# FFN input projection on one NeuronCore: the two blocks multiplied in full give way to first products of seven pairs ahead

## The chip, the cores and the metric

The kernel runs on 1 core of one Trainium2 chip. A core has a matrix engine (TensorE, PE in the profile), a vector engine (VectorE, DVE), a scalar engine (ScalarE, ACT), GpSimd (POOL), and a sync engine (SyncE, SP) that issues nearly all DMA transfers here. Each engine works through its own instruction list in the order in which the program was written, and the engines wait for each other by semaphores. The metric is the device time of one execution in microseconds (us); less is better.

## The reference, cut to what matters

One decoder block on 1024 tokens of width 1024: RMS norm and input projection, a dilated attention mixer and a convolution mixer, merged and projected (the "mix" projection), then a SwiGLU FFN with a hidden width of 2816. The change lies where the mix ends and the FFN begins:

```python
x = x + rms_norm(merged @ w_mix_out[l], g_post_mix[l])
h = rms_norm(x, g_pre_ffn[l])
gate, up = jnp.split(h @ w_ffn_in, 2, axis=-1)       # 2 x 2816 columns
x = x + rms_norm((jax.nn.silu(gate) * up) @ w_ffn_out, g_post_ffn[l])
```

All values are float32. The kernel splits a float32 operand into a rounded high part and a low part (`split`, `both`, `part`: a ScalarE copy makes the high part, a VectorE subtraction the low part) and replaces each product by three: high x high, high x low, low x high.

## The kernel before, in words

**Stages around the change.** Eight mix tiles of 128 tokens come first (loop with line 1697): tiles 0 and 1 together, then 2 to 7 one by one, each into two PSUM banks; one tile is 48 matrix products of 512 columns. The weights of all eight contraction steps (16 slots) and the left operands stay in SBUF until tile 7 is done. After each tile `mix_norm` runs beside the following products: squares (L1396), the first norm and the residual (L1403, L1407), a store of the new x (L1414), the second norm (L1418, L1420), which gives `hn`. After tile 3 the four `hn` of the first 512 tokens are transposed on TensorE in eight groups of four (L1428), scaled (L1434) and split (`split`, L1286 and L1287); after tile 7 the same is done for the last 512 tokens.

**The FFN input.** It runs over 22 blocks j of 128 hidden columns, each with a gate and an up half. From j = 2 on a block is one pair of weight tiles: `winograd` treats the 2 x 2 blocks (gate/up by first/second half of the contraction) and 2 x 2 halves of the activations (halves of the contraction by halves of the tokens) with 7 block products in place of 8. Each block product is `prod`: 4 contraction steps of 3 matrix products (lines 334 to 336). It needs sums of weights (`quarters`, steps 0 to 5) and sums T1 to T4 of the activations (`quarter_sums`, L391 to L401), which need all 1024 tokens. Blocks j = 0 and 1 are multiplied in full (`ffn_half`): 8 `unit` calls of 24 matrix products each (lines 318 to 320), the first four with the first 512 tokens alone.

**What sets the order.** The program order is written by hand. After every three matrix products of `unit` and `prod` (and every three or six of the mix) `tick()` is called; `later(n, step)` emits a step n ticks on, and background generators (`bg`) are advanced one step a tick unless they have yielded a number of ticks to skip. What is emitted at a tick stands at that place in the list of its engine. `load_ahead` issues weight loads on SP's queue. Slots: 42 tiles of 128x1024 (`slot`, NSLOT), 3 of the same size for rows (`ring`), 11 of half that size (`half`), and the 8 PSUM banks. A tile's slot comes free after its last use in program order, and what takes the slot next waits for that use.

Of the kernel before, what the change touches and what calls it, by code (L numbers as in the profile page):

```python
# [40 lines left out]

EARLY = 1

PLAIN = 2

LAST = 5
NSLOT = 42
# [11 lines left out]
def f(ap):  # L59
    return ap.bitcast(F32)  # L60


class Build:
# [104 lines left out]
    def flush(self, i):  # L168
        while any(p[0] <= i for p in self.pieces):
            self.one_piece()  # L170

    def load_ahead(self, i):
        while self.sent < min(len(self.jobs), i + 1):
# [3 lines left out]
            self.nc.sync.dma_start(self.raw[j][:, :n], src)  # L177
            self.sent += 1
# [33 lines left out]
    def quarters(self, i, c):  # L212


        nc = self.nc
        if c == 0:
            self.hl[i] = {}
        o = self.hl[i]
        r1, r2 = self.raw[i - 1], self.raw[i]
        a11, a12, a21, a22 = r1[:, :H], r1[:, H:], r2[:, :H], r2[:, H:]  # L220
        add = self.wsplit.tensor_tensor
        l, r = slice(0, H), slice(H, 2 * H)
        if c == 0:
            h, w = self.both(r1)
            o["A11"], o["A12"] = (h[:, l], w[:, l]), (h[:, r], w[:, r])
        elif c == 1:
            self.s12 = self.ring()
            add(self.s12[:, l], a21, a22, op=OP.add)
            add(self.s12[:, r], self.s12[:, l], a11, op=OP.add)  # L229
        elif c == 2:  # L230
            h, w = self.both(self.s12)
            o["S1"], o["S2"] = (h[:, l], w[:, l]), (h[:, r], w[:, r])
        elif c == 3:
# [3 lines left out]
            self.s12 = None  # L237
        elif c == 4:
            h, w = self.both(self.s34)
            o["S3"], o["S4"] = (h[:, l], w[:, l]), (h[:, r], w[:, r])  # L240
            self.s34 = None
        else:
            x = self.slot(F32R)
            nc.scalar.copy(x[:, l], a22)
            add(x[:, r], a22, f(x[:, l]), op=OP.subtract)
            o["A22"] = (x[:, l], x[:, r])
            del self.raw[i], self.raw[i - 1], self.hl[i]

    def queue_split(self, i):
        while self.queued < min(self.sent, i + 1):  # L250
# [88 lines left out]
    def winograd(self, W, T, f11, f12, f21, f22):  # L339
# [31 lines left out]
        self.prod(X, W["A22"], T["T4"], False, True)  # L371
        if rest:
            rest()
        f21(X)

    def quarter_sums(self, B, blocks):
# [906 lines left out]
    def split(self, src, n):  # L1283
        nc = self.nc
        s = self.slot(F32R)
        nc.scalar.copy(s[:, :n], src)  # L1286
        nc.vector.tensor_tensor(s[:, 512:512 + n], src, f(s[:, :n]), op=OP.subtract)  # L1287
        return s

    def rhs(self, ops):  # L1290
        return lambda kt: (ops[kt][:, :512], ops[kt][:, 512:])
# [118 lines left out]
    def mix_norm(self, tt, banks, x):  # L1410
        nc = self.nc
        x2 = self.ring()
        yield from self.residual(banks, x, self.g_mix, x2)
        nc.sync.dma_start(self.d_x2[tt], x2)  # L1414
        yield 1
        hn = self.slot()
        ss = self.tiny(4, "ss", 4)
        nc.scalar.activation(hn, x2, AF.Square, scale=ROOT, accum_out=ss[:, 0:1])  # L1418
        r = self.rstd_rows(ss[:, 0:1], self.eps_rms)
        nc.scalar.activation(hn, x2, AF.Copy, scale=r)  # L1420
        self.hn[tt // 4].append(hn)
        if tt % 4 == 3:
            yield 8
            op, y = [], None
            for kt in range(8):
                ps = self.bank("s")
                for i in range(4):
                    nc.tensor.transpose(ps[:, i * 128:(i + 1) * 128], self.hn[tt // 4][i][:, kt * 128:(kt + 1) * 128], self.ident)  # L1428
# [4 lines left out]
                y = x[:, (kt % 2) * H:(kt % 2 + 1) * H]  # L1433
                nc.scalar.activation(y, ps, AF.Copy, scale=self.col(C_PREF + kt))  # L1434
                self.h2f[tt // 4].append(y)
                yield 1
            op.append(self.split(y, H))
            self.h2[tt // 4] = op
            self.hn[tt // 4] = None

    def row_gain(self, src):
        g = self.slot()
# [4 lines left out]
def build(ctx, tc, aps):  # L1447
# [5 lines left out]
    def job(src, n=1024, kind=""):  # L1453
        J.append((src, n, kind))
        return len(J) - 1

    NQ, NK = 0, 12
    NU, NG, NGA, NGC = 24, 32, 40, 48
    def pair(a, b):
# [10 lines left out]
          for hg in range(2) for g in range(3)}  # L1470
# [4 lines left out]
    fi = [(job(aps["w_fi"][j], kind="row1" if j >= PLAIN else ""),  # L1475
           job(aps["w_fi"][FT + j], kind="row2" if j >= PLAIN else "")) for j in range(FT)]
# [147 lines left out]
    for n, hf in [(n, hf) for hf in range(2) for n in range(3)] + [(n, hf) for n in range(3, 8) for hf in range(2)]:  # L1624
# [2 lines left out]
            mg[n] = nxt  # L1627
            nxt = gate_load(B.d_gc[n + 1]) if n < 7 else (gate_load(B.d_ga[0]), gate_load(B.d_gc[0]))
        if B.tags["g"] == 2 and B.weighed == 4:
            B.banks(g=6, s=2)  # L1630
# [13 lines left out]
    for e in B.merges:  # L1644
        B.finish(e)
    if B.tags["g"] == 2:
        B.banks(g=6, s=2)
    mop = [[None] * 8, [None] * 8]

    rest = lambda: None  # L1650
# [18 lines left out]
    rest()  # L1669
    B.OT = None  # L1670

    W = [B.weights(mx[0])]
    B.g_mix = B.row_gain(aps["g_mix_row"])
    B.hn, B.h2, B.h2f = [[], []], [None, None], [[], []]
    norms = []

    def load_x(tt):
# [6 lines left out]
    xt = {0: load_x(0), 1: load_x(1)}  # L1684
    for tiles in ((0, 1), (2,), (3,), (4,), (5,), (6,), (7,)):
        banks = {tt: (B.bank(), B.bank()) for tt in tiles}
        for kt in range(KT):
            if len(W) == kt:
                B.ahead = int(kt < KT - 1)
                W.append(B.weights(mx[kt]))  # L1690
            for tt in tiles:
                m = mop[tt // 4]
# [48 lines left out]
            sub(s4, a12, a11, op=OP.subtract)  # L1741
            spill(p, "S4", s4)

    def ffn_half(j, hf, W):
        o = B.half()
        ps = B.unit(W[0], B.rhs(B.h2[hf]), KT)
        nc.scalar.activation(o, ps, AF.Silu)
        ps = B.unit(W[1], B.rhs(B.h2[hf]), KT)
        nc.vector.tensor_tensor(o, ps, o, op=OP.mult)
        held[j, hf] = o  # L1750

    B.wsplit = nc.vector
    Ws = []
    for j in range(PLAIN):
        Ws.append((B.weights(fi[j][0]), B.weights(fi[j][1])))
        ffn_half(j, 0, Ws[j])
    B.finish(norms[-1])
    B.g_mix = None
    h2 = [[(x[:, :H], x[:, H:]) for x in y] for y in B.h2]
    qs = B.bg(B.quarter_sums(B.h2f, (h2[0][:4], h2[0][4:], h2[1][4:])))  # L1760
    h2 = None
    for j in range(PLAIN):
        ffn_half(j, 1, Ws[j])
        Ws[j] = None
    B.summed = lambda: None
    B.first_sums(qs)
    B.h2 = B.h2f = None
    for j in range(0, PLAIN, 2):
        def plain_sums(n, p=j // 2, q=[held.pop((j + e, hf)) for e in range(2) for hf in range(2)]):
            if n == 0:  # L1770
                sums(p, q[0], None, q[1], None)
            elif n == 1:
                sums(p, q[0], None, q[1], q[3])
                q[1] = q[3] = None
            else:
                sums(p, q[0], q[2], None, None)
                q.clear()

        for n in range(3):
            B.later(6 + 5 * n + j, lambda n=n, f=plain_sums: f(n))  # L1780


    NP = FT // 2
    ORDER = (("A11", "B11"), ("A12", "B21"), ("S2", "T2"), ("S1", "T1"), ("S4", "B22"), ("S3", "T3"), ("A22", "T4"))
# [62 lines left out]
            splits(k)  # L1847
            yield 3

    for j in range(PLAIN, FT):  # L1850
        s = [None, None]
        p, odd = divmod(j, 2)

# [28 lines left out]
                held[0] = s[0]  # L1882
                sums(p, held[0], None, held[1], None)

        w = B.pair(fi[j][1])
        if j == FT - 1:
            for k in range(LEAD):
                loads(k)
            B.bg(first())
        B.winograd(w, B.T, f11, f12, f21, f22)  # L1890
        w = None
    B.T = None
    gain = B.row_gain(aps["g_ffn_row"])
# [190 lines left out]
```

## Time and profile before

| What | us |
|---|---|
| median of 3 runs (1691.92 to 1695.13) | 1693.91 |
| the profiled execution, its own time | 1690.83 |
| span of the profiled execution | 1689.0 |
| TensorE busy in it | 1676.4 (99%) |
| VectorE busy | 1259.8 (75%) |
| ScalarE busy | 818.9 (48%) |
| mix products, first to last (L1697) | 952.7 to 1043.9 |
| blocks j = 0 and 1 (L318 to L320) and the last transposes | 1043.9 to about 1092 |
| blocks j = 2 to 21 | about 1092 to 1472 |
| FFN output | 1472.2 to 1681.7 |

The times of a stage are counted from the first instruction of the span. A row of the profile names the line in the kernel, the engine, the operation, output and inputs by the program's names with buffer numbers left out (p is PSUM, b a slot, c a half, d a ring tile), and the shape; what stands in square brackets is the idle time of the engine before it and who ended it.

### The profile page before, as it was taken

The page shows a single profiled execution, that of the slowest core. Times are in us where ns is not written, and L with a number is a line of the kernel's source. Part 1 is how long each engine was busy: PE and PEld are TensorE (multiplying, and loading weights), DVE is VectorE, ACT ScalarE, POOL GpSimd, SP SyncE. Part 2 cuts the span into 40 slices and gives each one's busy share as a digit, 9 for nine tenths or more (in the row PEclk, how much of TensorE's full clock was granted, in tenths as well). Part 3 has the DMA queues.
Part 4 walks back from the last instruction along what each step waited for, and adds up shares of the span by engine and source line. Part 5 has one row for each costly group of instructions (what it writes and reads, how often), then busy time and mean ns, then how long its engine had stood idle before and what let it go on. Part 6 is the DMA issues. An engine that isn't in the chain of part 4 may idle for free.

```text
span 1689.0 us, 23464 instructions
## 1 busy us (share of the span) xinstructions
PE 1676.4 (99%) x8167; PEld 1403.7 (83%) x8167; DVE 1259.8 (75%) x2209; ACT 818.9 (48%) x1599; POOL 513.4 (30%) x399
## 2 busy tenths in 40 slices
PE   9999999999999999999999999999999999999998
PEld 7788888888888889999888888888888888888886
DVE  6789988788999777778886855765655566677686
ACT  6344334344444588888713456533333333354453
POOL 0017777888886265765200300000000000000000
PEclk9999999999999999999999999999999999999999
DMA  4252433455566987888998523032233222494334
GB/s 168 104 187 88 150 125 131 137 195 178 183 174 162 282 269 224 241 232 250 300 294 313 200 88 118 26 131 94 94 114 111 94 94 102 170 376 125 111 121 156
DMA packets 162563, 283.36 MB, mean 168 GB/s; under 512 B 47249, under 2 KB 78988, under 8 KB 162444
## 3 DMA queue, kind: packets, MB, share of 16 engines
q1 hardware_dynamic: 161948, 281.42, 51.1%
q8 instruction: 64, 1.05, 0.3%
q14 instruction: 55, 0.45, 0.1%
q0 software_dynamic: 352, 0.18, 0.1%
q10 hardware_dynamic: 144, 0.26, 0.0%
HBM read 191.10 MB, written 95.42 MB: 170 GB/s over the span
## 4 chain that ended last, share of the span: by engine, by line
PE 93%; DMA 3%; DVE 1%; POOL 1%; issue 1%; ACT 1%; SPq 0%; DVEq 0%; ACTq 0%; POOLq 0%
PE p L334 15%; PE p L335 15%; PE p L336 15%; PE p L1968 12%; PE p L966 5%; PE p L1697 5%; PE p L318 5%; PE p L320 5%; PE p L319 5%; PE p L967 3%; PE p L1082 2%; PE p L1153 2%; PE p L578 2%; PE p L1120 2%; DMA b<-dact 1%
## 5 line engine op out<-in xcount | busy, mean ns | idle before, releaser
L334 PE MATMUL p<-b,b 128*128 128x512 f32 x1204 | 468.7, 389 | 0.5 <-ACT c L353 0.3
L335 PE MATMUL p<-b,b 128*128 128x512 f32 x1204 | 468.4, 389 | 0.0
L336 PE MATMUL p<-b,b 128*128 128x512 f32 x1204 | 468.4, 389 | 0.0
L334 PEld LDWEIGHTS p<-b,b 128*128 128x128 f32 x1204 | 226.0, 188 | 48.6 <-DVE c L862 1.0
L336 PEld LDWEIGHTS p<-b,b 128*128 128x128 f32 x1204 | 226.0, 188 | 46.9
L335 PEld LDWEIGHTS p<-b,b 128*128 128x128 f32 x1204 | 226.0, 188 | 46.8
L1968 PE MATMUL p<-b,b 128*128 128x512 f32 x924 | 209.6, 389 | 0.0
L1968 PEld LDWEIGHTS p<-b,b 128*128 128x128 f32 x924 | 173.4, 188 | 36.0
L708 DVE SCALAR_TENSOR_TENSOR p<-b,par,p 128x511 f32<-128x511 f32 (+14 forms) x232 | 163.6, 740 | 0.0
L318 PE MATMUL p<-b,b 128*128 128x512 f32 x368 | 147.0, 399 | 0.0
L966 PE MATMUL p<-b,b 128*128 128x512 f32 x384 | 144.1, 407 | 0.0
L320 PE MATMUL p<-b,b 128*128 128x512 f32 x368 | 143.5, 390 | 0.0
L319 PE MATMUL p<-b,b 128*128 128x512 f32 x368 | 143.5, 390 | 0.0
L208 ACT CAST b<-d 128x1024 fp32r<-128x1024 f32 x86 | 90.6, 1054 | 105.2 <-POOL d L229 55.1
L209 POOL TENSOR_TENSOR b<-d,b 128x1024 fp32r<-128x1024 f32 x44 | 107.0, 2431 | 79.6 <-ACT b L208 72.3
L209 DVE TENSOR_TENSOR b<-d,b 128x1024 fp32r<-128x1024 f32 x42 | 51.3, 1222 | 101.1 <-ACT b L208 101.1
L1287 DVE TENSOR_TENSOR b<-b,b 128x512 fp32r<-128x512 f32 x133 | 92.5, 700 | 22.2 <-ACT b L1286 20.2
L967 PE MATMUL p<-b,b 128*128 128x256 f32 x384 | 107.7, 281 | 0.0
L1286 ACT CAST b<-b 128x512 fp32r<-128x512 f32 x133 | 82.3, 621 | 48.9 <-PE p L1968 18.6
L1095 ACT ACTIVATE c<-c,stat 128x128 f32<-128x128 f32 (+1 forms) x192 | 85.4, 449 | 13.4 <-DVE stat L1085 12.2
L1697 PE MATMUL p<-b,b 128*128 128x512 f32 x384 | 89.4, 391 | 0.0
L208 ACT CAST b<-b 128x1024 fp32r<-128x1024 f32 x47 | 49.6, 1054 | 81.4 <-POOL b L236 37.3
(233 smaller groups left out, 2915.1 us busy)
## 6 DMA issues: line engine op xcount, KB each, us to landing
b<-w_in SPq DMA_DIRECT2D x30, 512.0 KB, 4.9
dk<-c SPq DMA_DIRECT2D x48, 256.0 KB, 4.5
dq<-c SPq DMA_DIRECT2D x48, 256.0 KB, 3.5
b<-dq SPq DMA_DIRECT2D x48, 256.0 KB, 4.6
b<-dk SPq DMA_DIRECT2D x48, 256.0 KB, 6.8
b<-w_fi SPq DMA_DIRECT2D x24, 512.0 KB, 5.3
d<-w_in SPq DMA_DIRECT2D x23, 512.0 KB, 4.0
dqS<-c SPq DMA_DIRECT2D x44, 256.0 KB, 2.2
```

What stands on the lines that cost most here:

```text
L209: self.wsplit.tensor_tensor(lo, x, f(hi), op=OP.subtract)
L318: nc.tensor.matmul(ps, hi[:, s], a, start=kt == 0, stop=False)
L319: nc.tensor.matmul(ps, hi[:, s], b, start=False, stop=False)
L320: nc.tensor.matmul(ps, lo[:, s], a, start=False, stop=kt == nk - 1)
L334: nc.tensor.matmul(ps, hi[:, s], a, start=first and kt == 0, stop=False, skip_group_check=True)
L335: nc.tensor.matmul(ps, hi[:, s], b, start=False, stop=False, skip_group_check=True)
L336: nc.tensor.matmul(ps, lo[:, s], a, start=False, stop=kt == 3, skip_group_check=True)
L708: nc.vector.scalar_tensor_tensor(A[i][:, j:], src[i][:, :H - j], w[i], A[i][:, j:], op0=OP.mult, op1=OP.add)
L966: nc.tensor.matmul(ps, a, w, start=kt == 0, stop=kt == KT - 1, skip_group_check=True)
L967: nc.tensor.matmul(ps[:, 256:], b, w[:, :256], start=False, stop=kt == KT - 1, skip_group_check=True)
L1697: nc.tensor.matmul(banks[tt][nh], st, wt[:, nh * H:(nh + 1) * H], start=bool(kt == 0 and a), stop=bool(kt == KT - 1 and b))
L1968: nc.tensor.matmul(acc[t], x, y, start=first and e == 0, stop=last and e == 2, skip_group_check=True)
```

## The change

The two blocks in full are gone; all 22 blocks use 7 products. For blocks 0 to 6 the two products that need the first 512 tokens alone (A11 by B11, A12 by B21) are done right after mix tile 7 (`head`); each leaves an open sum in a PSUM bank and a first result in a half. Their weights are seven jobs of their own (`heads`: the gate row, loaded and split as plain weights), and the same gate row is loaded a second time with the pair. Then `tail` does the five products left of each of the seven pairs; the remaining 15 blocks go through `winograd` as before. The last 512 tokens are transposed tile by tile (`last_tokens`), and T1 to T4 are formed in part tile by tile, their last part and their splits behind tile 7. Loads of weights beyond the mix are held back (`limit`) until mix tile 7; the store of the new x is issued 5 ticks later than before; the pairs with heads load one pair further ahead; all 8 PSUM banks have one tag.

```diff
-PLAIN = 2
+HEAD = 7
@@ quarters(i, c)
         if c == 0:
+            if i in self.headed:
+                return
             h, w = self.both(r1)
@@ pair(i)
-        todo = [(1, lambda: self.quarters(i, 3)), (8, lambda: self.quarters(i, 4)), (10, lambda: self.quarters(i, 5))]
+        short = i in self.headed
+        a, b = (1, 8) if short else (8, 10)
+        todo = [(1, lambda: self.quarters(i, 3)), (a, lambda: self.quarters(i, 4)), (b, lambda: self.quarters(i, 5))]
+        if short:
+            todo = todo[1 + (i == self.headed[0]):]
         if n < len(J) and J[n][2] == "row1":
-            todo += [(LD, lambda: self.load_ahead(n + 1))]
-            todo += [(k, lambda c=c: self.quarters(n + 1, c)) for c, k in enumerate(PC)]
+            todo += [(14, lambda: self.load_ahead(n + 3))] if short else [(LD, lambda: self.load_ahead(n + 1))]
+            pc = PC if not short else (9, 9, 13, 17) if n + 1 in self.headed else (10, 12, 18)
+            todo += [(k, lambda c=c: self.quarters(n + 1, c)) for c, k in enumerate(pc)]
@@ new
+    def head(self, w, T, f11):
+        nc = self.nc
+        hi, lo = w
+        X, x1 = self.bank(), self.half()
+        self.prod(X, (hi[:, :H], lo[:, :H]), T["B11"], True, False)
+        nc.scalar.copy(x1, X)
+        Z = self.bank()
+        self.prod(Z, (hi[:, H:], lo[:, H:]), T["B21"], True, True)
+        return X, f11(Z, x1)
+
+    def tail(self, W, T, X, need, f11, f12, f21, f22):
...
+        need("T2")
+        self.prod(X, W["S2"], T["T2"], False, False)
+        nc.scalar.copy(x2, X)
+        V = self.bank()
+        need("T1")
+        self.prod(V, W["S1"], T["T1"], True, False)
+        nc.scalar.copy(v1, V)
+        need("T3")
+        self.prod(X, W["S3"], T["T3"], False, False)
+        f22(X, v1)
+        f11()
+        need("B22")
+        self.prod(V, W["S4"], T["B22"], False, True)
+        rest = f12(V, x2)
+        need("T4")
+        self.prod(X, W["A22"], T["T4"], False, True)
+        rest()
+        f21(X)
@@ mix_norm
-        nc.sync.dma_start(self.d_x2[tt], x2)
+        self.later(5, lambda: nc.sync.dma_start(self.d_x2[tt], x2))
...
+        if tt > 3:
+            yield from self.last_tokens(tt, hn)
+            return
@@ new
+    def last_tokens(self, tt, hn):
...
+        yield 9 if tt == 6 else 9 if tt < 6 else 9
+        for q in range(2):
+            ps = self.bank()
+            for i in range(4):
+                kt = 4 * q + i
+                nc.tensor.transpose(ps[:, i * 128:(i + 1) * 128], hn[:, kt * 128:(kt + 1) * 128], self.ident)
...
+            for i in range(4):
+                kt = 4 * q + i
+                d = two(self.raw2[kt // 2])[:, kt % 2 * 128:kt % 2 * 128 + 128]
+                if tt < 7 or i % 2 == 0:
+                    nc.scalar.activation(d, ps[:, i * 128:(i + 1) * 128], AF.Copy, scale=self.col(C_PREF + kt))
+                else:
+                    nc.vector.tensor_scalar(d, ps[:, i * 128:(i + 1) * 128], self.col(C_PREF + kt), None, op0=OP.mult)
+            yield 0
...
+        for i in range(2):
+            add(two(b11[i]), two(b11[i]), two(b12[i]), op=OP.subtract)
+        if tt > 5:
+            t2 = self.t2
+            for i in range(2):
+                stt(two(t2[i]), two(b11[i]), -1.0, two(b22[i]), op0=OP.mult, op1=OP.subtract)
+        if tt < 7:
+            yield 0
+            for i in range(2):
+                add(two(b12[i]), two(b22[i]), two(b12[i]), op=OP.subtract)
+            return
...
+        yield from keep("T2", list(t2))
+        yield from keep("T1", b11)
+        for i in range(2):
+            add(two(b12[i]), two(b22[i]), two(b12[i]), op=OP.subtract)
+        yield 0
+        yield from keep("T3", b12)
+        yield from keep("B22", b22)
+        for i in range(2):
+            stt(two(b21[i]), two(t2[i]), -1.0, two(b21[i]), op0=OP.mult, op1=OP.subtract)
+        yield 5
+        yield from keep("T4", b21)
@@ build, mix loop
+    B.limit = mx[-1]
...
+        if tiles[0] == 7:
+            B.limit = 1 << 30
+            for n, j in enumerate(heads):
+                B.later(max(8 * n - 4, 2), lambda j=j: B.load_ahead(j))
+                for c in range(2):
+                    B.later(8 * n + (5, 8)[c] + (2 if n > 1 else 0), lambda j=j, c=c: B.part(j, c))
+            B.later(19, lambda: B.load_ahead(fi[0]))
+            B.later(16 + 8 * HEAD - 6, lambda: B.load_ahead(fi[1]))
+            for c, n in ((0, 25), (1, 25), (2, 60), (3, 69), (4, 72)):
+                B.later(n, lambda c=c: B.quarters(fi[0], c))
+            B.wsplit = nc.vector
+            B.later(12, lambda: B.bg(B.early_sums()))
+            B.later(26, B.fourth)
@@ build, behind the mix: ffn_half, quarter_sums' call and plain_sums are gone
+    for j in range(HEAD):
+        f11, *rest = outs(j)
+        B.flush(heads[j])
+        X, r = B.head(B.hl.pop(heads[j]), B.T, f11)
+        todo.append((X, rest, r))
...
+    def need(name):
+        while len(B.T[name]) < 4:
+            next(norms[-1][0])
+    for j in range(FT):
+        w = B.pair(fi[j])
...
+        if j < HEAD:
+            X, rest, r = todo[j]
+            B.tail(w, B.T, X, need, r, *rest)
+        else:
+            B.finish(norms[-1])
+            B.winograd(w, B.T, *outs(j))
```

`keep(name, x)` in `last_tokens` splits four operands of one sum, 1 and 2 ticks apart by turns. `early_sums` forms T2 for tiles 4 and 5, `fourth` the part of T4 that tiles 4 to 6 allow. `two(x)` is one tile's 256 columns.

More of the change, by code (lines that the diff above doesn't have):

```diff
@@ L170, in flush @@
             self.one_piece()
+    limit = 1 << 30
+    headed = ()
     def load_ahead(self, i):
+        i = min(i, self.limit)
         while self.sent < min(len(self.jobs), i + 1):
@@ L232, in quarters @@
             o["S1"], o["S2"] = (h[:, l], w[:, l]), (h[:, r], w[:, r])
+            if self.s34 is not None:
+                self.s12 = None
         elif c == 3:
@@ L236, in quarters @@
             add(self.s34[:, r], self.s12[:, r], a12, op=OP.add)
[L237 removed]
+            if "S2" in o:
+                self.s12 = None
         elif c == 4:
@@ L1439, in mix_norm, with two, keep @@
-            self.hn[tt // 4] = None
+            op = [(a[:, :H], a[:, H:]) for a in op]
+            self.T = dict(B11=op[:4], B21=op[4:], B22=[], T1=[], T2=[], T3=[], T4=[])
+            self.hn[0] = None
+    def last_tokens(self, tt, hn):
+        nc = self.nc
+        o = (tt - 4) * 128
+        if tt == 4:
+            self.raw2 = [self.slot() for _ in range(4)]
+        def two(x):
+            return x[:, 2 * o:2 * o + 256]
+        add, stt = nc.vector.tensor_tensor, nc.vector.scalar_tensor_tensor
+        yield 9 if tt == 6 else 9 if tt < 6 else 9
+        for q in range(2):
+            ps = self.bank()
+            for i in range(4):
+                kt = 4 * q + i
+                nc.tensor.transpose(ps[:, i * 128:(i + 1) * 128], hn[:, kt * 128:(kt + 1) * 128], self.ident)
+            if q == 1:
+                hn = None
+            for i in range(4):
[5 more added lines that the diff above has]
+                    nc.vector.tensor_scalar(d, ps[:, i * 128:(i + 1) * 128], self.col(C_PREF + kt), None, op0=OP.mult)
+            ps = None
+            yield 0
+        if tt < 7:
+            yield 3
+        b11, b12, b21, b22 = self.raw1[:2], self.raw2[:2], self.raw1[2:], self.raw2[2:]
+        for i in range(2):
[4 more added lines that the diff above has]
+                stt(two(t2[i]), two(b11[i]), -1.0, two(b22[i]), op0=OP.mult, op1=OP.subtract)
+        if tt < 7:
+            yield 0
+            for i in range(2):
+                add(two(b12[i]), two(b22[i]), two(b12[i]), op=OP.subtract)
+            return
+        T = self.T
+        self.raw1 = self.raw2 = self.g_mix = None
+        def keep(name, x):
+            for k in range(4):
+                y = self.split(self.feature(x[k // 2], k), H)
+                T[name].append((y[:, :H], y[:, H:]))
+                if k % 2:
+                    x[k // 2] = None
+                yield (1,2)[k%2]
+        yield from keep("T2", list(t2))
[7 more added lines that the diff above has]
+            stt(two(b21[i]), two(t2[i]), -1.0, two(b21[i]), op0=OP.mult, op1=OP.subtract)
+            t2[i] = None
+        yield 5
+        yield from keep("T4", b21)
@@ new lines, in fourth, with early_sums @@
+    def fourth(self):
+        for x, y in zip(self.t2, self.b21):
+            self.nc.vector.scalar_tensor_tensor(y[:, :768], x[:, :768], -1.0, y[:, :768], op0=OP.mult, op1=OP.subtract)
+    def early_sums(self):
+        b11, b22 = self.raw1[:2], self.raw2[2:]
+        self.t2 = [self.slot() for _ in range(2)]
+        for i in range(2):
+            a, b, c = (x[i][:, :512] for x in (self.t2, b11, b22))
+            self.nc.vector.scalar_tensor_tensor(a, b, -1.0, c, op0=OP.mult, op1=OP.subtract)
+            yield 1
@@ L1455, in job, with pair2 @@
         return len(J) - 1
+    def pair2(j):
+        job(aps["w_fi"][j], kind="row1")
+        return job(aps["w_fi"][FT + j], kind="row2")
     NQ, NK = 0, 12
@@ L1474, in build @@
     mx = [job(aps["w_mx"][j]) for j in range(8)]
-    fi = [(job(aps["w_fi"][j], kind="row1" if j >= PLAIN else ""),
-           job(aps["w_fi"][FT + j], kind="row2" if j >= PLAIN else "")) for j in range(FT)]
+    heads = [job(aps["w_fi"][j]) for j in range(HEAD)]
+    fi = [pair2(j) for j in range(FT)]
+    B.headed = [fi[j] for j in range(HEAD)]
     B.d_conv = [B.dram.tile([128, 1024], F32, name=f"dconv{b}") for b in range(8)]
@@ L1629, in build @@
         if B.tags["g"] == 2 and B.weighed == 4:
-            B.banks(g=6, s=2)
+            B.banks(g=8)
         ps = B.unit(ws[n], conv_rhs(hf), KT)
@@ L1646, in build @@
     if B.tags["g"] == 2:
-        B.banks(g=6, s=2)
+        B.banks(g=8)
     mop = [[None] * 8, [None] * 8]
@@ L1742, in sums @@
             spill(p, "S4", s4)
[L1744 to L1750, printed above, removed]
-    B.wsplit = nc.vector
[L1753 to L1780, printed above, removed]
+    B.wsplit = nc.vector
     NP = FT // 2
@@ L1848, in first, with outs @@
             yield 3
-    for j in range(PLAIN, FT):
+    def outs(j):
         s = [None, None]
```

42 lines of the change are left out of this document (28 added, 14 removed).

## The prediction

> **What bounds the kernel now.** I read the page first (busy shares, the chain that ended last, the costliest groups), then the windows of the stretch that changes, then the timelines of TensorE, ScalarE and VectorE there.
>
> ```profile
> PE 1676.4 (99%) x8167; PEld 1403.7 (83%) x8167; DVE 1259.8 (75%) x2209; ACT 818.9 (48%) x1599; POOL 513.4 (30%) x399
> PE 93%; DMA 3%; DVE 1%; POOL 1%; issue 1%; ACT 1%; SPq 0%; DVEq 0%; ACTq 0%; POOLq 0%
> L334 PE MATMUL p<-b,b 128*128 128x512 f32 x1204 | 468.7, 389 | 0.5 <-ACT c L353 0.3
> L318 PE MATMUL p<-b,b 128*128 128x512 f32 x368 | 147.0, 399 | 0.0
> ```
>
> The first row alone proves little, since a matmul row overlaps the next one. The chain does: 93% of it runs through TensorE. The last two rows are products of `prod` and of `unit`; the last column, the idle time before them, is 0.5 and 0.0 us. So the FFN input has no gap to win: what counts there is the number of products.
>
> The windows (start:end, their length, then busy time and count for PE, PEld, DVE, ACT, POOL, the granted clock, the DMA share and GB/s) say the same and give the price of a product:
>
> ```profile
> 1044.00:1082.00 38.00, 38.00 (x185) 31.50 (x184) 26.37 (x48) 26.84 (x44) 0.00 (x0) 1.00 0.21 77
> 1091.00:1110.00 19.00, 19.00 (x85) 15.76 (x84) 17.17 (x26) 8.73 (x13) 0.00 (x0) 1.00 0.22 84
> 1289.00:1472.00 183.00, 183.00 (x809) 151.53 (x808) 106.65 (x145) 64.59 (x94) 0.00 (x0) 1.00 0.30 109
> 800.00:820.00 20.00, 17.71 (x117) 15.21 (x116) 18.13 (x58) 16.76 (x54) 9.78 (x12) 1.00 1.04 316
> ```
>
> 183.00 us for 809 products of 512 columns is 0.226 us each, start to start (the 389 ns of a row include the pipeline). A tick, three products, is 0.68 us; a `prod` of twelve is 2.71 us. The second row matters below: VectorE 90% busy and TensorE still without a gap.
>
> **The change part by part.**
>
> *Products.* Before: two blocks in full, 8 units x 24 = 192 products, and 20 blocks x 7 x 12 = 1680, together 1872. After: 7 heads x 2 x 12, 7 tails x 5 x 12 and 15 blocks x 7 x 12 = 1848. 24 fewer, 24 x 0.226 = **5.4 us less** on the engine that sets the end. The transposes stay 64.
>
> *Where they stand.* From the timeline of TensorE:
>
> ```profile
> 1008.49 0.60 PE L1428 MATMUL p<-ident,b 128*128 128x128 f32 x4
> 1008.84 1.64 PE L1697 MATMUL p<-b,b 128*128 128x512 f32 x6
> 1010.32 0.60 PE L1428 MATMUL p<-ident,b 128*128 128x128 f32 x4
> 1019.84 0.66 PE L1428 MATMUL p<-ident,b 128*128 128x128 f32 x4 [0.21 <-ACT b L1434]
> 1022.07 22.04 PE L1697 MATMUL p<-b,b 128*128 128x512 f32 x96
> 1043.94 0.39 PE L318 MATMUL p<-b,b 128*128 128x512 f32 x1
> ```
>
> A group of four transposes and six products takes 1010.32 - 1008.49 = 1.83 us, so the group costs 1.83 - 6 x 0.226 = 0.47 us. Before, the last eight groups stand among the full blocks, after them stand two per tile; moved, not added: 0 us. The 0.21 us wait on a bank of its own tag (two banks) can go with the common tag; I count 0.
>
> *First seam: tile 6's transposes.* `last_tokens(6)` is forced out right behind mix tile 7 and ahead of the first head, and TensorE takes it in order. So its `hn` must be there when tile 7 ends. Tile 7's loop takes 48 x 0.226 = 10.85 us plus tile 5's two groups, 0.94: it ends 11.8 us after tile 6. Tile 6's chain before:
>
> ```profile
> 1033.04 0.60 ACT L1396 ACTIVATE d<-p 128x512 f32<-128x512 f32 x1
> 1036.83 1.28 DVE L1407 TENSOR_TENSOR d<-d,c 128x512 f32<-128x512 f32 x2
> 1038.21 1.06 ACT L1418 ACTIVATE b<-d 128x1024 f32<-128x1024 f32 x1 [3.57 <-DVE d L1407]
> 1040.55 1.15 ACT L1420 ACTIVATE b<-d,rr 128x1024 f32<-128x1024 f32 x1 [0.87 <-DVE rr L1388]
> 1040.36 0.16 DVE L1388 TENSOR_TENSOR rr<-rr 128x1 f32<-128x1 f32 x1
> ```
>
> `hn` is complete at 1041.70, 8.7 us after the tile's end at 1033.0; 3.1 us to spare. But the change puts new work into this chain. The load of head 0 is emitted at tick 2 of tile 7 and its first split at tick 5, between the chain's L1403 (ticks 3, 4) and L1407 (ticks 5, 6): on ScalarE the copy, on VectorE the subtraction, and both queues stand until the load has landed. It can't be earlier: I count 16 weight slots, 8 left operands, 1 gain, 8 + 4 operands of the first half, 4 raw tiles of the second and 1 `hn` = 42, all of NSLOT, so SP waits for the first contraction step of tile 7 (some 1 to 1.4 us in).
>
> ```profile
> L177 SPq DMA_DIRECT2D b<-w_fi x24: 328/406/745, 953.1 to 1437.6; - x24
> DMA to landing us min/median/max: 4.0/4.8/5.8
> ```
>
> The load lands at 1.2 + 4.8 = 6.0 us (ends 5.0 and 7.2). Then copy, subtraction, two L1407 (starts 0.6 us apart, together 2.5), and the 3.5 us from the end of L1407 (1038.11) to that of `hn`, and about 0.2 for sums of tile 5 between: landing + 6.2 = 12.2 us against 11.8. **+0.4 us** (ends 0 and 1.6). The Trainium skill (DMA: Bandwidth & Descriptors, Anatomy of one DMA) gives a fixed 2.0 us plus bytes by 436 GB/s, by its fit, made for transfers that GpSimd issues, an estimate of 3.2 us for 512 KB; the trace's least, 4.0, disagrees. By the page the load lands at 4.4 and this term is 0, the sum -5.0 us in place of -4.6.
>
> *Second seam: tile 7's transposes*, at tick 35 counted from tile 7's start, i.e. 19 ticks x 0.68 = 12.9 us of heads after tile 6's groups. The chain of 8.7 us starts late, behind eight 128-wide ScalarE copies of tile 6 (each under the 0.60 of a 128x512 row; I take 0.3, together 2.4 us). VectorE has 2.4 us of other work in it (a split, a head's sum, pair 0's first two sums), of which 1.25 lie beside ScalarE's square: 2.4 + 8.7 + 1.1 = 12.2 us. 0 us taken (ends 0 and 1).
>
> *The head window*, ticks 16 to 72, 56 x 0.68 = 38.1 us. VectorE's durations:
>
> ```profile
> L1287 DVE TENSOR_TENSOR b<-b,b 128x512 fp32r<-128x512 f32 x133 | 92.5, 700 | 22.2 <-ACT b L1286 20.2
> L209 DVE TENSOR_TENSOR b<-d,b 128x1024 fp32r<-128x1024 f32 x42 | 51.3, 1222 | 101.1 <-ACT b L208 101.1
> L1403 DVE SCALAR_TENSOR_TENSOR d<-p,rr,b 128x512 f32<-128x512 f32 x16 | 11.3, 745 | 0.2
> L540 DVE TENSOR_TENSOR b<-b,b 128x256 fp32r<-128x256 f32 x12 | 4.5, 422 | 0.0
> ```
>
> Ten weight splits, seven head sums and fourteen operand splits at 0.70 (21.7), tile 7's norm 4.7 (two L1403, two L1407, eleven small ones), twelve 256-wide sums at 0.42 (5.0), four small scalings 1.2, `fourth` two 768-wide at about 0.95 (1.9), pair 0's steps 1 to 3 two, one and two instructions (4.0): 38.5 us of rows in 38.1 us. Tight, but rows overlap: the two L1407 above take 1.28 us together, so they start some 0.60 apart, and the window needs some 34 us, 90%, the share of the second window row, where TensorE had no gap. The queue runs late by some 2.7 us about tick 40 and has caught up at tick 50. What waits for it: the split of the next head's weights (emitted 6 ticks, 4 us, ahead), and PSUM. Seven open sums and one Z fill the eight banks: the Z of head 6 needs head 5's sum (L1855's twin) done within one `prod`, 2.7 us, and tail 0's V needs head 6's, behind a 1.2 us split. **+0.2 us** (ends 0 and 2.7, one `prod`).
>
> *Tails.* Per 20 ticks, 13.6 us: VectorE two 1024-wide and about eleven 512-wide rows, 10 us; ScalarE 5 us; loads of 1 MB and 0.9 MB of spills, 140 GB/s, under the 316 of the 800 row. T2, T1, T3 and B22 are all emitted by tick 75, used from 72, 76, 80, 84: in time. T4 is forced at tick 88 with two of four splits open, their VectorE part behind the sum that reads V: the third operand comes at about +1.5 us, its low part is wanted at 1.36 + 0.23 = 1.59. **+0.2 us** (ends 0 and 1.4, two splits).
>
> *Loads and stores.* Seven gate rows are read twice, 3.7 MB, in a window with DMA share 0.21: off the path. SP takes the store of x (5 ticks later) between loads; what stood behind it before:
>
> ```profile
> SPq L1414 <- DVE d L1407: 81.4, 8, 25.8
> ```
>
> That is 81.4 us of SP waiting for L1407 at a store emitted too early; issued later, loads behind it go earlier. Nobody waited for them: 0 us. The FFN output loads its first spilled blocks 5 steps ahead, unchanged.
>
> *Sum:* -5.4 + 0.4 + 0.2 + 0.2 = **-4.6 us**, on the profiled execution 1690.83 to 1686.2. The median of the runs stands 3.1 us above that execution, so 1693.91 - 4.6 = **1689.3 us**, -0.27%. With all bounds: -5.6 (the 0.21 gained) to +1.3.
>
> **The rivals.**
>
> *A, the seams take the gain back:* first and second seam at their upper ends and a bank wait (1.6 + 1 + 1) leave -1.8 us, 1692.1, no measurable change. For it: the first chain has no slack by the sum above, the head window's VectorE is full. Against: 90% busy was covered before.
>
> *B, slower: the first split holds tile 6's norm.* Each us that head 0's load lands after 5.6 us costs one us of TensorE at the first seam. If the load gets a slot that is free only at the end of tile 7 (11.8 us), it lands at 16.6, the stall is 11 us, and the result -5.4 + 11 = +5.6 us, 1699.5. It decides from a landing at 11.0 us (no gain) and 14.4 us (slower by 0.2%). For it: no slot is spare, two engines and SP queue in order. Against: three slots come free at each step of tile 7, the oldest would be taken.
>
> The clock could add to B: the 800:820 row has 2.29 us without TensorE work and a granted clock of 1.00, so a short wait does not lower it. The Trainium skill (TensorE: Matmul & The Clock Gate, Part 1) says an idle window of about 3.4 us halves the clock until a busy one has passed; by it B would pay some 1.7 us more, 1701, and A nothing. No idle time that long is in the rows shown.
>
> *C, the saving is swallowed later:* if the FFN output waited for spills or loads, the end would not move, 1693.9. Against: its products follow each other, and VectorE's spills only move with the stage.
>
> **How the numbers follow.** About 0.2% (3.4 us) is what a measurement of this kernel can tell from no change. Forecast 0.62: faster by 3.4 to 5.6 us, 1688.3 to 1690.5. A and C together 0.22, within 0.2%. B or a like wait 0.16, slower. Forecast's own range with a run spread of 1 us: 1687.5 to 1691.5; to leave out no more than two in ten the range reaches over A to 1695.
>
> **What would show it.** The chain that ended last enters the FFN output here:
>
> ```profile
> 1472.19 209.45 PE p L1968 x924
> ```
>
> Right: TensorE products without an idle row from the mix to the FFN output; that row 4.6 us earlier, at 1467.6; 304 rows of `unit` in place of 368 for each of its three lines and 1260 of `prod` for 1204. First seam: idle time before a transpose behind mix tile 7, released by ScalarE's `hn`, and on ScalarE a copy of head 0's weights released by a load of w_fi, at about 6 us after tile 6. Head window: idle before a Z or V product, released by VectorE. T4: idle before the last product of tail 0. The prediction is wrong if the idle rows there add up to more than 2 us, or if none is there and the end still doesn't move.

## The result, and the profile after

The changed kernel takes 1686.45 us (median of 11 runs, 1685.55 to 1690.6), the kernel before beside it 1691.88 us (median of 11 runs, 1690.2 to 1695.13). The ratio is 0.997 with a 95% interval of 0.9961 to 0.998: faster by 0.2 to 0.39%. The profiled execution has a span of 1684.4 us against 1689.0.

The page of the changed kernel (its lines have moved: `prod` is L350 to L352, `unit` L334 to L336, the FFN output L2115):

```profile
PE 1672.0 (99%) x8143; PEld 1400.5 (83%) x8143; DVE 1269.6 (75%) x2241; ACT 819.6 (49%) x1626; POOL 512.0 (30%) x398
L350 PE MATMUL p<-b,b 128*128 128x512 f32 x1260 | 490.8, 390 | 0.5 <-ACT c L369 0.3
L334 PE MATMUL p<-b,b 128*128 128x512 f32 x304 | 121.3, 399 | 0.0
L2115 PE MATMUL p<-b,b 128*128 128x512 f32 x924 | 209.7, 389 | 1.5 <-DVE c L2002 1.5
```

1260 and 304 rows for each of three lines are the 24 products fewer. The last row is new: the FFN output, which followed the last block without idle time, now waits 1.5 us once. The end of the chain of waits of the changed kernel shows where (start, length):

```profile
1466.25 0.57 issue
1466.82 0.69 DVE c L2002
1467.56 209.75 PE p L2115 x924
```

L2002 is VectorE's last read of the last block's open sum in PSUM.

I compare one stretch, from the start of the first mix product to that of the first FFN output product, so that what happens ahead of the mix (its start lies between 951.9 and 955.6 in the executions below, with nothing changed there) drops out. By the rows of these two lines, TensorE's first products start at 952.7 and 1472.0 before, at 952.1 and 1467.6 after:

| | stretch, us |
|---|---|
| before | 519.3 |
| after | 515.5 |
| after, in a second profile (run 9) | 515.3 |
| 24 products at 0.226 us | -5.4 |
| the new wait: 1.5 idle and 0.16 in which the next product would have started | +1.7 |
| the rest (a 0.2 us wait before a transpose is gone, 0.12 us in the first tail is new) | -0.1 |

The seams cost nothing that can be seen. Tile 6's chain in the changed kernel (timelines of SP, ScalarE, VectorE and TensorE, in order of time; L194 and L195 are the split of head 0's weights, L1466 and L1479 the former L1407 and L1420, L1520 the transposes, L1527 their scaling):

```profile
1034.09 2.15 SPq L181 DMA_DIRECT2D b<-w_fi  x3
1036.32 2.18 ACT L1527 ACTIVATE b<-p,par 128x128 f32<-128x128 f32 x8 [1.80 <-PE p L1520]
1038.33 1.19 ACT L194 CAST b<-b 128x512 fp32r<-128x512 f32 x2
1039.04 0.69 DVE L195 TENSOR_TENSOR b<-b,b 128x512 fp32r<-128x512 f32 x1 [2.24 <-ACT b L194]
1039.65 1.29 DVE L1466 TENSOR_TENSOR d<-d,c 128x512 f32<-128x512 f32 x2
1043.31 1.16 ACT L1479 ACTIVATE b<-d,rr 128x1024 f32<-128x1024 f32 x1 [0.87 <-DVE rr L1447]
1044.73 1.04 PE L1520 MATMUL p<-ident,b 128*128 128x128 f32 x8
```

VectorE stands 2.24 us at the split with L1466 behind it, and the normalised rows are complete at 1044.47, 0.26 us before TensorE wants them. A window over the heads, and one from within the first tail (which begins at 1084.7) into the second:

```profile
1045.00:1083.00 38.00, 38.00 (x177) 31.60 (x175) 34.35 (x70) 24.75 (x54) 0.00 (x0) 1.00 0.31 114
1089.00:1102.60 13.60, 13.48 (x60) 10.81 (x59) 10.93 (x16) 8.20 (x12) 0.00 (x0) 1.00 0.10 38
```

VectorE is busy 34.35 us of 38.00 in the heads and TensorE never stops; in the second window TensorE is idle 0.12 us, in the first tail, at the second product of T4's third operand.

### The profile page after: what moved, and what is told of

Read it like the earlier page. It is cut to its first block, busy times and chain, and to the rows that moved or that the text cites. A ratio compares the mean times of both kernels' runs of the same rounds, so it can differ in the third digit from the quotient of the medians.

```text
span 1684.4 us, 23503 instructions
## 1 busy us (share of the span) xinstructions
PE 1672.0 (99%) x8143; PEld 1400.5 (83%) x8143; DVE 1269.6 (75%) x2241; ACT 819.6 (49%) x1626; POOL 512.0 (30%) x398
## 3 DMA queue, kind: packets, MB, share of 16 engines
q8 instruction: 64, 1.05, 0.3%
## 4 chain that ended last, share of the span: by engine, by line
PE 93%; DMA 3%; DVE 1%; ACT 1%; POOL 1%; issue 1%; DVEq 0%; ACTq 0%; POOLq 0%; SPq 0%
PE p L350 16%; PE p L351 16%; PE p L352 16%; PE p L2115 12%; PE p L1018 5%; PE p L1859 5%; PE p L334 4%; PE p L335 4%; PE p L336 4%; PE p L1019 3%; PE p L1134 2%; PE p L630 2%; PE p L1205 2%; PE p L1172 2%; DMA b<-dact 1%
## 5 line engine op out<-in xcount | busy, mean ns | idle before, releaser
L350 PE MATMUL p<-b,b 128*128 128x512 f32 x1260 | 490.8, 390 | 0.5 <-ACT c L369 0.3
L352 PE MATMUL p<-b,b 128*128 128x512 f32 x1260 | 490.2, 389 | 0.0
L350 PEld LDWEIGHTS p<-b,b 128*128 128x128 f32 x1260 | 236.5, 188 | 50.7 <-DVE c L914 1.0
L351 PEld LDWEIGHTS p<-b,b 128*128 128x128 f32 x1260 | 236.5, 188 | 49.5 <-DVE b L1342 0.5
L352 PEld LDWEIGHTS p<-b,b 128*128 128x128 f32 x1260 | 236.5, 188 | 49.1
L2115 PE MATMUL p<-b,b 128*128 128x512 f32 x924 | 209.7, 389 | 1.5 <-DVE c L2002 1.5
L2115 PEld LDWEIGHTS p<-b,b 128*128 128x128 f32 x924 | 173.3, 188 | 37.9 <-DVE c L2002 1.9
L212 ACT CAST b<-d 128x1024 fp32r<-128x1024 f32 x83 | 87.2, 1050 | 94.1 <-POOL d L235 55.1
L213 POOL TENSOR_TENSOR b<-d,b 128x1024 fp32r<-128x1024 f32 x44 | 106.9, 2429 | 79.7 <-ACT b L212 72.3
L334 PE MATMUL p<-b,b 128*128 128x512 f32 x304 | 121.3, 399 | 0.0
L336 PE MATMUL p<-b,b 128*128 128x512 f32 x304 | 118.5, 390 | 0.0
L213 DVE TENSOR_TENSOR b<-d,b 128x1024 fp32r<-128x1024 f32 x39 | 47.6, 1221 | 79.6 <-ACT b L212 79.6
L212 ACT CAST b<-b 128x1024 fp32r<-128x1024 f32 x49 | 51.6, 1052 | 84.3 <-POOL b L244 37.3
```

The lines of the kernel that those rows point to most:

```text
L213: self.wsplit.tensor_tensor(lo, x, f(hi), op=OP.subtract)
L334: nc.tensor.matmul(ps, hi[:, s], a, start=kt == 0, stop=False)
L336: nc.tensor.matmul(ps, lo[:, s], a, start=False, stop=kt == nk - 1)
L350: nc.tensor.matmul(ps, hi[:, s], a, start=first and kt == 0, stop=False, skip_group_check=True)
L351: nc.tensor.matmul(ps, hi[:, s], b, start=False, stop=False, skip_group_check=True)
L352: nc.tensor.matmul(ps, lo[:, s], a, start=False, stop=kt == 3, skip_group_check=True)
```

## The experiments

Times are medians, each beside the kernel before; "stretch" is as above, in each run's one profiled execution.

**1. Is it the bank?** In the changed kernel the pool of the FFN output gives the bank of the last block's open sum to its first sum. One word gives those first sums other banks:

```diff
     B.banks(y=4, x=4)
-    B.bank("y")
+    B.bank("x")
```

> The changed kernel with one edit: the PSUM pool of the FFN output is first asked for a bank of tag x instead of tag y, so that its first four sums take other banks than the last block's open sum. Bank theory (the 1.5 us wait of the first FFN output product comes from the bank that the last block's X has just used): the wait goes to 0.2 us or less, the span falls from 1684.4 to about 1682.9, the time is 6.0 to 6.9 us under the kernel before. Rival (the product waits because VectorE is late with the sums in general): the wait stays at 1.5 us and the span at 1684.4.

1684.55 us, ratio 0.9959 (0.9945 to 0.9972), span 1682.7, stretch 513.7. No wait before the FFN output is left among TensorE's waits. Before's 519.3 - 5.4 = 513.9: with the wait gone the saving is the 24 products. (Rows don't number the banks; that it is this one bank is concluded from the edit.)

**2. The tag alone.** The kernel before with one tag for all banks behind the attention and nothing else:

```diff
-                ps = self.bank("s")
+                ps = self.bank()
...
-            B.banks(g=6, s=2)
+            B.banks(g=8)
...
-        B.banks(g=6, s=2)
+        B.banks(g=8)
```

> The kernel before with the one part of the change alone that gives all PSUM banks one tag (behind the attention, and for the transposes). Bank theory: the first FFN output product now waits about 1.5 us for a VectorE read of the last block's sum, as in the changed kernel, and the 0.2 us wait before a transpose at 1019.8 goes: 1.0 to 1.5 us slower than before, no change by the bound of 0.2%. Rival (the wait belongs to the new order of the blocks): no such wait, 0 to -0.2 us.

1692.66 us, ratio 1.0006 (0.9998 to 1.0015), stretch 520.5, 1.2 us longer. The timed difference alone is not clear of no change; the stretch and a new row show it. TensorE's list of waits in this kernel has

```profile
PE p L1968 <- DVE c L1877: 1.5, 1, 1.5
```

at its head, which the kernel before has not. So the wait belongs to the tag, not to the order of the blocks. The likely reason, not shown by itself, is that with two banks of another tag set aside the pool that follows has banks that the last block didn't use.

**3 and 4. The first seam.** Head 0's weights are loaded twice into the same tile, so that they land one load later; in run 4 the two splits are also emitted behind tile 6's second norm:

```diff
                 B.later(max(8 * n - 4, 2), lambda j=j: B.load_ahead(j))
+                if n == 0:
+                    B.later(2, lambda j=j: nc.sync.dma_start(B.raw[j][:, :1024], J[j][0]))
                 for c in range(2):
-                    B.later(8 * n + (5, 8)[c] + (2 if n > 1 else 0), lambda j=j, c=c: B.part(j, c))
+                    B.later(10 + c if n == 0 else 8 * n + (5, 8)[c] + (2 if n > 1 else 0), lambda j=j, c=c: B.part(j, c))
```

(the last two lines in run 4 alone)

> The changed kernel, head 0's weights loaded twice, the second time into the same tile behind the first, so that they land one load (about 4.1 us) later. Seam theory (the first split stands between the two halves of tile 6's norm in the queues of ScalarE and VectorE, and tile 6's transposes are first on TensorE behind mix tile 7, with 0.3 us to spare): TensorE idles 3.5 to 3.9 us before tile 6's transposes, the span grows from 1684.4 to about 1688. Rival (other slack takes it up): no idle time there, span 1684.4 to 1685.

> As the run before (the load one load later), but head 0's two splits are emitted at ticks 10 and 11 in place of 5 and 8, behind tile 6's second norm. Seam theory (queue order, not the load itself): no idle time before tile 6's transposes or the first head, span 1684.4 to 1684.8, and tile 6's normalised rows ready about 3 us before they are used. Rival (the load's lateness counts by itself, head 0 waits for its weights): 2 us or more of idle time before the first head.

Run 3: 1689.81 us, ratio 0.9992 (0.9983 to 1.0001), stretch 517.6, 2.1 us longer than the changed kernel's. Its timelines:

```profile
1036.55 0.33 SPq L181 DMA_DIRECT2D b<-w_fi  x1
1039.80 0.33 SPq L1839 DMA_DIRECT2D b<-w_fi  x1
1043.14 1.14 ACT L194 CAST b<-b 128x512 fp32r<-128x512 f32 x2 [2.18 <-DMA b<-w_fi]
1043.80 0.69 DVE L195 TENSOR_TENSOR b<-b,b 128x512 fp32r<-128x512 f32 x1 [4.53 <-ACT b L194]
1048.07 1.15 ACT L1479 ACTIVATE b<-d,rr 128x1024 f32<-128x1024 f32 x1 [0.87 <-DVE rr L1447]
1049.27 1.09 PE L1520 MATMUL p<-ident,b 128*128 128x128 f32 x8 [1.92 <-ACT b L1479]
```

The second load goes out when the first has landed, 3.25 us after it, and lands 3.3 us on. ScalarE waits for it, VectorE for ScalarE, the norm behind them, and TensorE for the norm: the mechanism as expected, the size not (1.9 us of 3.5 to 3.9). A load takes 0.8 us less here than I reckoned, and in the changed kernel the split had not waited for its load at all in the end: the load, issued at 1034.09, landed after 3.3 us, at 1037.4, and the copy starts straight behind eight scalings of tile 5's transposes (1038.33, no idle time), which cover part of the delay. In run 3 the copy starts at 1043.14, with the mix 2.5 us later 2.3 us behind the changed kernel's; less the 0.26 us to spare that is 2.05 us, which fits the stretch (2.1 longer) and the idle row of 1.92.

Run 4: 1687.8 us, ratio 0.9977 (0.9967 to 0.9987), stretch 515.4, as the changed kernel. The load is as late, the norm no longer stands behind it:

```profile
1040.86 1.15 ACT L1479 ACTIVATE b<-d,rr 128x1024 f32<-128x1024 f32 x1 [0.87 <-DVE rr L1447]
1041.92 2.17 ACT L194 CAST b<-b 128x512 fp32r<-128x512 f32 x4
1044.86 1.04 PE L1520 MATMUL p<-ident,b 128*128 128x128 f32 x8
```

The rows are complete at 1042.01, 2.85 us ahead. So it is the place in the queues, not the load, that decides this seam.

**5 and 6. How many heads.**

```diff
-HEAD = 7
+HEAD = 6
...
-            for c, n in ((0, 25), (1, 25), (2, 60), (3, 69), (4, 72)):
+            for c, n in ((0, 25), (1, 25), (2, 52), (3, 61), (4, 64)):
```

(run 6: 5 heads, and 44, 53, 56)

> The changed kernel with 6 heads in place of 7 (the weight sums of block 0 are moved 8 ticks forward with the first tail). The number of products is the same. Cover theory (the heads hide the chain of the last tokens, whose last part, T4, is formed 62 ticks after mix tile 7): the splits of T4 are forced behind the sum that reads V, 1.3 to 3 us of idle time on TensorE in the first tail, span 1685.7 to 1687.4. Rival (six cover it; the seventh only takes a PSUM bank): 0 to 0.3 us, span 1684.4 to 1684.7.

> The changed kernel with 5 heads in place of 7, the weight sums of block 0 moved 16 ticks forward. Cover theory: T3 and B22 are forced too, and TensorE waits 4 to 7 us in the first tail, span 1688 to 1691, about the gain of the change. Rival (five cover it): below 0.5 us.

Six: 1690.04 us, ratio 0.9989 (0.9979 to 0.9998), stretch 517.3. Five: 1692.72 us, ratio 1.0009 (1.0 to 1.0019), stretch 518.7. The first tail waits for the forced splits. Six heads, timeline and windows (the number behind the five engines is the granted clock):

```profile
1093.36 0.50 PE L350 MATMUL p<-b,b 128*128 128x512 f32 x1 [1.46 <-ACT b L1341]
1094.19 0.61 PE L351 MATMUL p<-b,b 128*128 128x512 f32 x1 [0.33 <-DVE b L1342]
```

```profile
1089.00:1092.00 3.00, 2.90 (x13) 2.06 (x11) 1.87 (x3) 2.00 (x3) 0.00 (x0) 1.00 0.00 0
1092.00:1093.40 1.40, 0.04 (x1) 0.04 (x1) 1.40 (x4) 0.71 (x2) 0.00 (x0) 1.00 0.00 0
1093.40:1095.00 1.60, 1.27 (x3) 0.78 (x4) 1.60 (x4) 1.60 (x4) 0.00 (x0) 0.82 0.00 0
1095.00:1097.00 2.00, 2.00 (x6) 1.59 (x5) 2.00 (x4) 0.40 (x1) 0.00 (x0) 0.50 0.00 0
1097.00:1099.00 2.00, 2.00 (x8) 1.60 (x8) 1.15 (x3) 1.05 (x1) 0.00 (x0) 0.79 0.00 0
```

1.8 us of waiting, and then a lower clock: by the last three windows 0.18 x 1.6 + 0.50 x 2.0 + 0.21 x 2.0 = 1.7 us more, the price of one half for 3.4 us. The stretch grows only by 1.8, because the wait before the FFN output is 0.2 in place of 1.5 us (that the last block's banks fall differently with one head fewer is my reading, not shown). The waits were as expected, the span of 1688.2 not (1685.7 to 1687.4): the clock was not in the reckoning. The median lies 3.3 us above that of run 7, measured on the same chip with the changed kernel's stretch, so 1.5 us more than the profiled stretch shows. Of the eleven executions six have a mean granted clock of 0.998 or less over the whole program, in run 7 two of ten; where it fell is not known for those without a trace. With five heads the first tail has waits of 0.60, 0.19, 0.96, 1.30 and 0.39 us, 3.4 together, at full clock. Expected were 4 to 7; the direction holds, the size was high. The median is 6.0 us above run 7's and the stretch 3.2; the profiled execution, 1690.38, is the shortest of the ten, and six of them have a mean clock of 0.998 or less. Seven heads just cover the last tokens' chain.

**7. The store.**

```diff
-        self.later(5, lambda: nc.sync.dma_start(self.d_x2[tt], x2))
+        nc.sync.dma_start(self.d_x2[tt], x2)
```

> The changed kernel with the one part undone that holds the store of the new rows back by 5 ticks. By the prediction's term of 0: no change of the span beyond 0.3 us, though the loads of the heads 2 to 4 are issued some 6 us later. Rival (SP's queue stood in the way of the heads' loads): idle time on TensorE before a head of 1 us or more.

1686.76 us, ratio 0.9976 (0.9967 to 0.9985), stretch 515.4: no difference to the changed kernel. Nobody was waiting for what stands behind the store.

**8. The loads one pair further ahead.**

```diff
-            todo += [(14, lambda: self.load_ahead(n + 3))] if short else [(LD, lambda: self.load_ahead(n + 1))]
+            todo += [(LD, lambda: self.load_ahead(n + 1))]
```

> The changed kernel with the one part undone that loads the pairs with heads one pair further ahead: the load is issued 2 ticks after the pair before begins, 7 ticks (4.8 us) ahead of its first sum, in place of 15 ticks (10.2 us). Theory of the prediction (loads are hidden): VectorE waits up to 1 us at that sum in each tail, TensorE does not, span within 0.3 us of 1684.4. Rival (the sums then come too late for the next tail): 0.5 to 1 us of idle time in each of six tails, span 1687 to 1690.

1691.57 us, ratio 1.0005 (0.9995 to 1.0015), stretch 520.8: the whole gain gone. (The profiled execution, 1695.03, is a long one, with the mix starting 3.5 us later than in the changed kernel.) Both theories of the expectation missed: VectorE waits longer and TensorE stops longer, in fewer places. TensorE stops in three of the tails, and VectorE's list of waits over the tails (1080 to 1200) is led by the loads:

```profile
1127.82 0.50 PE L350 MATMUL p<-b,b 128*128 128x512 f32 x1 [0.95 <-DVE c L1985]
1156.33 0.50 PE L350 MATMUL p<-b,b 128*128 128x512 f32 x1 [0.78 <-DVE c L1985]
1186.27 0.50 PE L350 MATMUL p<-b,b 128*128 128x512 f32 x1 [2.21 <-DVE c L1985]
```

```profile
DVE d L234 <- DMA b<-w_fi: 20.5, 5, 4.2
```

L234 is the first weight sum of the next pair. VectorE stands up to 4.2 us at it, and L1985, which reads PSUM for the present tail, stands behind it; TensorE needs that bank. That is so in the first two stops (4.18 and 4.01 us). In the third and longest VectorE stands 4.29 us at a split (L213) ahead of L234 and L1985, for a ScalarE copy (L212) that itself waited 2.73 us for the pair's other load: the same cause by way of ScalarE. A stop costs more than its idle row: the windows around these three have 85, 85 and 78 products where the changed kernel has 90 each, 22 x 0.226 = 5.0 us for 3.9 us of idle rows. The row counts from the end of a product, 0.16 us (0.389 - 0.226) after the next could have started, and the first product after a stop takes 0.50.

**9 and 10. Both edits.** The changed kernel again, and beside it the bank order of run 1 with the split order of run 4.

> The changed kernel as it is, once more, as the neighbour of the next run on one chip: 4.5 to 6 us under the kernel before, a wait of 1.5 us before the first FFN output product.

> The changed kernel with two edits: the bank order of the first experiment, and head 0's splits at ticks 10 and 11, behind tile 6's second norm. Theory: the first edit takes the 1.5 us wait away, the second changes no time (tile 6's rows have 0.3 us to spare already, with it about 3 us): 1.2 to 1.8 us under the changed kernel beside it, mix start to FFN output start 513.5 to 514. Rival (the 0.3 us to spare are used up in some executions): a further gain and a smaller spread of the runs.

The changed kernel: 1686.91 us, ratio 0.9974 (0.9963 to 0.9985). With both edits: 1684.68 us, ratio 0.9958 (0.9945 to 0.997), stretch 513.7, as with the bank order alone; the tile 6 rows have 2.85 us to spare (complete at 1041.65, transposes at 1044.50). By the stretch the second edit changes nothing, and run 1 and run 10 lie 1.6 to 1.8 us under the changed kernel. The medians of runs 9 and 10 differ by 2.2, a little more than the 1.2 to 1.8 expected, and the executions of run 10 lie closer together (1.1 us between the extremes of five, 2.6 of seven in run 9), which were the rival's signs. But its condition is not seen: in the profiles of the changed kernel and of runs 1, 7 and 9 the rows have 0.25 to 0.27 us to spare every time. Five executions can't settle it.

## Why the prediction was right or wrong

The direction and the main mechanism were right: 24 products at 0.226 us, 5.4 us. But the measured time, 1686.45, lies under the stated range. That the FFN output's first product starts at 1467.56, where 1467.6 was written, is luck: the sum counted 0.8 us for seams and tails that cost next to nothing and 0 for the tag, which cost 1.7, and the mix happened to start 0.6 us earlier in this execution. The stretch fell by 3.8 us, not 4.6.

- *The base.* The step that failed for the range is "The median of the runs stands 3.1 us above that execution", with "a run spread of 1 us". Three runs spanning 3.2 us gave 1693.91; eleven gave 1691.88, 1.05 us above the profiled execution, and they span 4.9 us. From that base the same sum says 1687.3; 2.0 of the 2.85 us by which the prediction was high are this. Part of the spread goes with the granted clock: of the kernel before's 24 executions beside runs 1 to 4, those with a mean granted clock of 0.999 have a median of 1690.58 us (15), with 0.998 of 1692.2 (7), with 0.997 of 1693.91 (2), some 1.7 us for 0.001, which is 0.001 of the time. (Within one clock reading there is a spread too: the 15 lie between 1689.59 and 1693.81.) The profiled execution, at 0.999, was the nearer base with its own 1690.83; the sum on it says 1686.2. The clocks of the three runs are not on record. The other 0.8 us are partly open: the medians fell by 5.4 us where the stretch fell by 3.8. In the set of run 9 the executions at 0.999 alone have medians of 1690.87 before and 1686.89 after, 4.0 apart, as its stretch says; so the clock may be the rest.
- *Products:* right. Run 1 shows the full 5.4 us (519.3 to 513.7, with the 0.2 us wait before a transpose gone too).
- *First seam, +0.4:* measured 0, with 0.26 us to spare. The chain was right to the part (landing + 6.2 us predicted; in run 3 6.1 from the start of the first copy), the load's 4.8 us was too long: it took 3.3. What was left out is that ScalarE's eight scalings of tile 5 stand ahead of the copy; the copy starts behind them, 0.9 us after the landing; without that the margin would have been some 1.2 us in place of 0.26.
- *The 3.2 us by the Trainium skill.* For this load the estimate from the fit of the Trainium skill (DMA: Bandwidth & Descriptors, Anatomy of one DMA) was nearer than the rows that I preferred: 3.3 us measured in the changed kernel, 3.25 and 3.3 in run 3, all issued by SyncE. None of these had a load issued shortly ahead of it. The rows' 4.0 to 5.8 us are from loads of which most went out in pairs some 0.5 us apart; that this makes the difference was not tested by itself.
- *Second seam, 0:* right. Rows complete at 1057.34, 12 us behind tile 6's transposes as reckoned, wanted at 1058.56.
- *Head window, +0.2:* measured 0; "some 34 us" of VectorE was 34.35.
- *Tails, +0.2:* 0.12 us at T4.
- *The tag, "I count 0":* this failed. I looked at the tag only where it could free a wait, not at who takes over the banks. It cost 1.7 us (run 1 takes 1.8 away; run 2 adds 1.2, with the 0.2 us wait before a transpose gone).
- *Loads, "off the path":* the time was right, the reason not. The loads are hidden only because they are issued 15 ticks ahead; run 8 gives the price if that cover is gone, 5.3 us, which the prediction should have named.
- *Rival B:* its mechanism and its rate are borne out by run 3: the load landed 7.75 us after tile 6's end (1035.39), 2.15 past rival B's 5.6, and the stretch grew by 2.1. Its condition did not occur: head 0's load went out at 1034.09, early in tile 7, so the slot was an early one. The remark beside it that a short wait does not lower the clock was too general: its 2.29 us were two waits, of 1.02 and 1.27, and in run 5 stops of 1.46 and 0.33 us were followed by half the clock.
- *Rivals A and C:* not so; the seams took nothing, and the saving arrives at the end less one new wait.

## What to carry to other kernels

Where one engine is busy without a gap, count its instructions; that number was right to 0.1 us, and everything else was whether the rest keeps up. When buffers are pooled anew (a tag, a bank order), ask which buffer the next stage gets first and who read it last. And put work that waits for a load behind the chain that is due next in the same engine's queue, not between its halves: a load that is "hidden" holds up everything behind its first reader.

## What the runs showed of the hardware that I had not expected

- After 1.46 us of idle time and a second stop of 0.33 us, with one product between, the granted clock fell to 0.50, for 3.4 us by the reckoning above (run 5). TensorE's rows show the same: products start 0.43 us apart in place of 0.226 from 1094.19 to 1097.58. In run 3 one stop of 1.92 us left it at 1.00, as did 2.29 us in two waits in the window 800 to 820 of the kernel before, and the five stops of run 6, among them 1.30 and 0.39 us with one product between. The Trainium skill (TensorE: Matmul & The Clock Gate, Part 1) speaks of a free-running window of about 3.4 us: after an idle one the clock is half, after a busy one full again. The half clock and how long it lasted agree with that, but a full window without work was not needed in run 5. What decided it is open.
- A stop of TensorE costs 0.2 to 0.4 us more than the idle time in its row (the changed kernel and run 8).
- Part of the spread of this kernel's times goes with the mean granted clock of the execution, some 1.7 us between the medians for each 0.001 (the kernel before beside runs 1 to 4, as above).
- A 512 KB load with none issued shortly ahead of it landed in 3.25 and 3.3 us (run 3, the changed kernel); the loads of these weights in the kernel before, mostly in pairs, in 4.0 to 5.8.
